# A two-layer attention trunk on one core: the first chunk's activations loaded already transposed, and the first loads reordered

## The chip, the cores and the metric

The kernel runs on one core of one Trainium2 chip. The metric is the device time of one execution in microseconds (us), less is better; the number to be predicted is the median of several runs.

## What is computed

The reference is a decoder trunk of two layers on 256 tokens of width 1024, in float32. Each layer does, in essence:

```
h = rms_norm(x, g_pre_mix[l])
parts = split(h @ w_in[l])                       # 2848 columns: q, k, v of two head groups, gates
o_nsa = nsa_mixer(...)                           # compressed, selected and window attention, gated
o_fox = fox_mixer(...)                           # attention with forgetting gates
x = x + rms_norm(concat(o_nsa, o_fox) @ w_out[l], g_post_mix[l])
h = rms_norm(x, g_pre_mlp[l])
x = x + rms_norm(square(relu(h @ w_up[l])) @ w_down[l], g_post_mlp[l])
```

For the products with `w_in` the kernel uses that the norm's factor is one number per token: it multiplies `(x * g) @ w_in`, and the factor is applied when a chunk's sums are read out of PSUM.

## The kernel before

**Tiling.** Tokens are two tiles t = 0, 1 of 128. The contraction dimension 1024 is eight slices k of 128. The columns of `w_in` are six chunks; the first that is worked on (chunk 0) has 512 columns, chunk 1 has 288, chunk 2 has 512, then three more. TensorE contracts over partitions, so the activations must stand with the contraction dimension on partitions: the tile pair `xT`, 128 x 8 x 256.

**Split precision.** Every operand is split into a part `hi` (float32r, made by ScalarE as a copy) and `lo` (VectorE, the value less `hi`). `mm3` (line 572) makes one product from three matmuls: hi·hi, hi·lo, lo·hi. Weights are split the same way in `Weights.get` (line 422): the load lands in `wraw`, ScalarE writes `whi`, VectorE writes `wlo`. There are RBUFS = 4 buffers for `wraw`, WBUFS = 7 each for `whi` and `wlo`, and 4 for the compression weights `w1`, which are used without a split.

**The start of layer 0.** Lines 515 to 534 issue the first loads, all on SyncE's queue (SP), in this order: the first half of token tile 0 of `x`; the identity (first 128 columns of `cst`); weight unit 0; `gcol`, the gain as eight columns; the second half of tile 0; units 1, 2, 3; the two halves of tile 1; units 4 to 7; the next columns of `cst`. A unit of chunk 0 is one k slice, 128 x 512 (`FIRSTS`, line 42). `first_xT(t)` (line 690) transposes tile t of `x` on TensorE, eight 128x128 transposes against the identity, four into each of two PSUM banks, multiplies by `gcol` into a tile `xg` (VectorE for t = 0, ScalarE for t = 1), and splits `xg` into `xT`. Some matmuls on a zeroed tile `warm` (line 537, WARM = 3, two instructions each) stand ahead of everything on TensorE.

Lines 1155 to 1161 run chunk 0 by token: all eight k of tile 0, then all eight of tile 1; `first_xT(1)` is recorded after the fourth product, the row factors `r_mix` after the eighth (`rstd_of_x`, line 601: ScalarE squares both halves of a tile of `x` with a sum, then a chain of small operations on VectorE and ScalarE gives one factor per token). `evac0` (line 736) reads chunk 0 out of PSUM with these factors into `kv_tok`, `kS` and `vS`. `row_scales` (line 1008) turns the factors into a row by four small matmuls. `gather_blocks` (line 805) transposes `kv_tok` and adds the position embedding on VectorE into `kstk` and `kstv`; `hidden_part` (line 822) multiplies these with `w1` in one stretch of 32 narrow matmuls, recorded behind the last quarter of chunk 2 (for k) and of chunk 3 (for v).

**Who sets the order.** The program is first recorded and then ordered by a planner, `Recorder.order` (line 241): for each engine it picks, at each point of its model's time, the ready operation with the smallest key (the place where it was recorded, or a key set by hand) for which buffers are free. A weight load has the key of the place 12 units earlier (`LOAD_LEAD`), a split that of one unit earlier. The order that comes out is fixed when the kernel is built, and each engine and SP's queue run it in order.

Of the kernel before, what the change touches and what calls it, by code (L numbers as in the profile page):

```python
# [18 lines left out]
F32 = mybir.dt.float32  # L19
F32R = mybir.dt.float32r  # L20
AF = mybir.ActivationFunctionType
OP = mybir.AluOpType
PSUM = bass.MemoryType.PSUM

P = 128
D = 1024
S = 256
NT = 2
# [5 lines left out]
LASTK = 4  # L34
LANE = 0.9
WAIT = 0.7
X1AT = 3
WARM = 3
RETILE = 145
SEQ = [(2, 0), (2, 1), (2, 2), (2, 3), (3, 0), (3, 1), (3, 2), (3, 3)]  # L40
EVKEY = 1
FIRSTS = [(i, i + 1) for i in range(8)]
UPK = 7
TOK, WBUFS, RBUFS = 6, 7, 4
LOAD_LEAD, SPLIT_LEAD = 12, 1
EPS = 1e-6
SEGS = ((0, 128, 0), (128, 384, 1))
GELU_C = 1.5957691216057308
# [1 line left out]
C_ID, C_ROPE, C_SID, C_TRI, C_MASK, C_CM, C_M01, C_ROW, C_SEL, C_END = np.cumsum(  # L50
    [0, 128, 64, 32, 256, 256, 32, 32, 8, 8]).tolist()
# [114 lines left out]
class Recorder:  # L166
    def __init__(self, nc, tc):
        self.nc, self.tc = nc, tc
        self.ops, self.fifo, self.key, self.hot, self.lane, self.group = [], {}, None, False, None, None
        for e in ("tensor", "vector", "scalar", "sync"):  # L170
            setattr(self, e, _Engine(self, e))

# [14 lines left out]
    def add(self, engine, name, args, kw):  # L187
        if self.group is not None:
            assert engine == "tensor"
            self.group.append((name, args, kw))  # L190
            return
        op = Op()
        op.engine, op.name, op.args, op.kw = engine, name, args, kw
        op.key = len(self.ops) if self.key is None else self.key
        if self.lane is not None and self.key is None:
            op.key = self.lane + LANE * (len(self.ops) - self.lane)
        op.urgent = self.hot
        views = []
        for _, a, k in args[2] if name == "stretch" else [(name, args, kw)]:
            views += [(i == 0, v) for i, v in enumerate(a) if isinstance(v, View)]  # L200
            views += [(i in ("out", "accum_out"), v) for i, v in k.items() if isinstance(v, View)]
        op.tile = _tile(op) if engine == "tensor" else None
        op.cost = _cost(op, views)
        deps = {}
        op.bufs = []
        for is_out, v in sorted(views, key=lambda x: x[0]):
            b, m = v.buf, v.mask()
            if b not in op.bufs:
                op.bufs.append(b)

            def against(entries):
                for o, p, q, bank in entries:
                    if o is not op and o not in deps and (
                            (bank and engine == "tensor") or
                            (p[0] < v.p[1] and v.p[0] < p[1] and (m & q).any())):
                        deps[o] = _latency(o, op)

            against(b.writes)
            entry = (op, v.p, m, is_out and b.psum and engine == "tensor")
            if is_out:  # L220
                against(b.reads)
                b.writes = [w for w in b.writes if not (
                    w[0] in deps and v.p[0] <= w[1][0] and w[1][1] <= v.p[1] and not (w[2] & ~m).any())]
                b.writes.append(entry)
            else:
                if b.psum:
                    for o, _, _, _ in b.reads:
                        if o.engine != engine and o is not op and o not in deps:
                            deps[o] = 130.0
                b.reads.append(entry)  # L230
        op.deps = deps
        for b in op.bufs:
            if not b.ops:
                self.fifo.setdefault(b.tag, []).append(b)
            b.ops += 1
        op.succs = []
        for d in deps:
            d.succs.append(op)
        self.ops.append(op)

    def order(self):
# [41 lines left out]
        while events:  # L283
# [5 lines left out]
            for e, ops in waiting.items():  # L289
                while busy[e] <= t:  # L290
# [35 lines left out]
                            count += 1  # L326
                            heapq.heappush(events, (best.end + (260 if b.psum else 150), count, b.tag))
                    for s in best.succs:
                        s.ready = max(s.ready, best.end + s.deps[best])
                        s.missing -= 1  # L330
                        if not s.missing:
                            waiting[s.engine].append(s)
                            count += 1
                            heapq.heappush(events, (s.ready, count, None))
# [74 lines left out]
class Weights:  # L409
# [12 lines left out]
    def get(self, i):  # L422
        nc, marks = self.nc, self.marks
        assert len(marks) == i
        marks.append(len(nc.ops))
        if i not in self.raw:
            nc.key = marks[max(i - LOAD_LEAD, 0)]
            self.load(i)
        kind, shape, src = self.units[i]
        raw = self.raw.pop(i)  # L430
        nc.key = None
        if kind == "raw":
            return raw
        nc.key = marks[max(i - SPLIT_LEAD, 0)]
        hi = self.tile([P] + shape, F32R, name="whi", tag="whi", bufs=WBUFS)
        lo = self.tile([P] + shape, F32R, name="wlo", tag="wlo", bufs=WBUFS)
        nc.scalar.activation(hi, raw, AF.Copy)
        nc.vector.tensor_sub(lo, raw, hi.bitcast(F32))
        nc.key = None
        return hi, lo  # L440

# [11 lines left out]
def trunk(nc, A, consts_in, out, sbp, pp):  # L453
    def tile(shape, dtype, name, tag=None, bufs=1):
        return nc.tile(sbp, shape, dtype, name, tag, bufs)

    def psum(tag):
        return nc.tile(pp, [P, 512], F32, tag, tag, {"acc": 2, "x": 2, "s": 3, "o": 1}[tag], psum=True)

    def small(shape, name, bufs=2):  # L460
        return tile(shape, F32, name=name, tag=name, bufs=bufs)
# [54 lines left out]
    cst = tile([P, C_END], F32, name="cst")  # L516
    ident = cst[:, C_ID:C_ID + P]
    xin = A["x"][0].rearrange("(t p) d -> t p d", p=P)
    gcol = tile([P, 8], F32, name="gcol")
    load_x = lambda t, n: nc.sync.dma_start(X[t][:, n * 512:n * 512 + 512], xin[t][:, n * 512:n * 512 + 512])  # L520
    load_x(0, 0)
    nc.sync.dma_start(cst[:, :P], consts_in[:, :P])
    W.load(0)
    nc.sync.dma_start(gcol, A["gcol"])
    load_x(0, 1)
    W.load(1)
    W.load(2)
    if len(FIRST) > 5:
        W.load(3)
    load_x(1, 0)  # L530
    load_x(1, 1)
    for i in range(3 + (len(FIRST) > 5), len(FIRST)):
        W.load(i)
    nc.sync.dma_start(cst[:, P:C_TRI], consts_in[:, P:C_TRI])


    warm = tokt("warm")
# [40 lines left out]
    def split(src, dst):  # L578
        nc.scalar.activation(dst[0], src, AF.Copy)
        nc.vector.tensor_sub(dst[1], src, dst[0].bitcast(F32))  # L580
# [106 lines left out]

    xT = new_xT()

    def first_xT(t):  # L690
        for n in range(2):
            ps = psum("s")
            for j in range(4):
                a = n * 512 + j * P
                nc.tensor.transpose(ps[:, j * P:j * P + P], X[t][:, a:a + P], ident)
            y = tokt("xg").rearrange("p (k n) -> p k n", k=4)
            for j in (0, 2):
                k = 4 * n + j
                if t:
                    for i in (j, j + 1):  # L700
                        nc.scalar.activation(y[:, i, :], ps[:, i * P:i * P + P], AF.Copy, scale=gcol[:, 4 * n + i:4 * n + i + 1])
                else:
                    nc.vector.tensor_mul(y[:, j:j + 2, :], ps[:, j * P:j * P + 2 * P].rearrange("p (k n) -> p k n", k=2),
                                         gcol[:, k:k + 2, None].to_broadcast([P, 2, P]))
                split(y[:, j:j + 2, :], [z[:, k:k + 2, t * P:t * P + P] for z in xT])

    first_xT(0)
    selr = tile([P, 8], F32R, name="selr")
    ident_r = tile([P, P], F32R, name="identr")
    r_mix = [None, None]  # L710
# [2 lines left out]
    for l in range(DEPTH):  # L713
        first = l == 0
        if first:
            params = load_params(0)
            nc.sync.dma_start(cst[:, C_TRI:], consts_in[:, C_TRI:])
        rows, bias, w2 = params
        smT = small([P, 37], "smT", 1)
        posT = {"k": smT[:, 0:16], "v": smT[:, 16:32]}  # L720
        b1T = smT[:, 32:36]
        b2k = smT[:, 36:37]
# [430 lines left out]


        if first:
            for n, _ in enumerate(in_chunk(0, evac0, by_token=True)):
                if n == X1AT:
                    first_xT(1)
                if n == 7:
                    for t in range(NT):  # L1160
                        r_mix[t] = rstd_of_x(t, "rm")
        else:

            for n, _ in enumerate(in_chunk(0, evac0, by_token=True)):
                if n == 6:
                    urgent(carry)
                    next(carry)
                    for t in range(NT):
                        r_mix[t] = rstd_of_x(t, "rm")
# [235 lines left out]
def layouts(a):  # L1405
# [7 lines left out]
    r["bias"] = np.concatenate([a["b_nsa_gate"], a["b_forget"], a["cmp_b2_v"]], axis=1)  # L1413
    w2 = [a[k].reshape(DEPTH, 2, P, 1, HD).transpose(0, 2, 1, 3, 4) for k in ("cmp_w2_k", "cmp_w2_v")]
    r["w2"] = np.stack([np.concatenate([x, x], axis=3) for x in w2], axis=2)
    r["gcol"] = a["g_pre_mix"][0].reshape(8, P).T
    r["consts"] = constants()
    return {k: np.ascontiguousarray(v) for k, v in r.items()}

# [15 lines left out]
```

## Time and profile before

| | |
|---|---|
| median of 3 runs | 648.28 us (647.78 to 648.38) |
| time of the profiled execution | 648.48 us |
| its span, first to last instruction | 646.7 us |
| TensorE busy | 634.1 us, 4032 matmuls |
| VectorE busy | 466.8 us |
| ScalarE busy | 358.7 us |
| read from HBM | 113.02 MB, 176 GB/s over the span |

The span lies inside the measured time; the rest (1.8 us) is around it. All times within the trace count from the start of the span. In its rows PE is TensorE's matmuls, PEld its weight loads, DVE is VectorE, ACT is ScalarE and SPq is SyncE's queue of DMA issues. An entry reads "out<-in", by the program's names of tiles; nearly every row bears the line of the planner's emitter, L348, so tiles tell the operations apart. Matmuls are pipelined: the duration of one is longer than the distance to the next, so the pace of TensorE is read from the starts.

### The profile page before, as it was taken

The numbers are of one execution on the slowest core, as the hardware profiler recorded it, in microseconds if no ns is written. First come the engines' busy times: TensorE is split into PE (matmuls) and PEld (weight loads), VectorE is DVE, ScalarE is ACT, GpSimd is POOL, SyncE is SP. The second block draws the span as 40 slices with busy tenths as digits, with TensorE's granted clock in tenths as the row PEclk, the third lists the DMA queues.
The fourth block names the chain that finished last, engine by engine and source line by source line (L and its number), as shares of the span: only waits on it lengthen the run. The fifth ranks groups of instructions, "written<-read, shape, count | busy, mean of one in ns | idle before, by whom it ended". The sixth has DMA issues, their size and how long they took to land.

```text
span 646.7 us, 10766 instructions
## 1 busy us (share of the span) xinstructions
PE 634.1 (98%) x4032; PEld 547.0 (85%) x4032; DVE 466.8 (72%) x1050; ACT 358.7 (55%) x681; POOL 0.2 (0%) x4
## 2 busy tenths in 40 slices
PE   8999999999999999999999999999999999999995
PEld 6788977778999899889888988777799899889984
DVE  5689999979965554555599799997987564555534
ACT  7557577654753553554366566764566543554332
POOL 0000000000000000000000000000000000000000
PEclk9999999999999999999999999999999999999999
DMA  8896915325775566655415973352277666555601
GB/s 260 272 325 211 326 50 178 116 66 192 236 256 193 176 186 196 188 181 186 121 51 159 329 223 104 115 170 76 74 240 245 193 193 189 181 185 195 189 7 65
DMA packets 53935, 114.75 MB, mean 177 GB/s; under 512 B 4274, under 2 KB 14716, under 8 KB 53884
## 3 DMA queue, kind: packets, MB, share of 16 engines
q1 hardware_dynamic: 53884, 114.08, 54.3%
q8 instruction: 31, 0.51, 0.3%
q14 instruction: 20, 0.16, 0.1%
HBM read 113.02 MB, written 1.05 MB: 176 GB/s over the span
## 4 chain that ended last, share of the span: by engine, by line
PE 93%; DMA 3%; DVE 2%; ACT 1%; issue 1%; SPq 0%; DVEq 0%
PE s L348 37%; PE acc L348 28%; PE x L348 24%; PE o L348 4%; DMA wraw<-in_w_in_dram 2%; DMA x<-in_x_dram 1%; DVE wlo L348 1%; ACT whi L348 0%; ACT xT L348 0%; DVE kstv L348 0%; SPq L348 0%; DVE kstk L348 0%; DVE xT L348 0%; ACT kS L348 0%; DVE m L348 0%
## 5 line engine op out<-in xcount | busy, mean ns | idle before, releaser
L348 DVE TENSOR_TENSOR wlo<-wraw,whi 128x1024 fp32r<-128x1024 f32 (+2 forms) x196 | 230.2, 1180 | 123.6 <-ACT whi L348 123.3
L348 ACT ACTIVATE whi<-wraw 128x1024 fp32r<-128x1024 f32 (+2 forms) x196 | 200.7, 1029 | 172.8 <-PE acc L348 74.1
L348 PE MATMUL s<-xT,whi 128*128 128x256 f32 x896 | 162.0, 283 | 0.0
L348 PEld LDWEIGHTS s<-xT,whi 128*128 128x128 f32 x896 | 139.9, 190 | 1.2
L348 PE MATMUL s<-xT,wlo 128*128 128x256 f32 x448 | 126.7, 283 | 0.0
L348 PE MATMUL acc<-whi,aT 128*128 128x512 f32 x256 | 89.3, 393 | 0.0
L348 PE MATMUL x<-whi,aT 128*128 128x512 f32 x256 | 88.9, 392 | 0.0
L348 PEld LDWEIGHTS s<-xT,wlo 128*128 128x128 f32 x448 | 85.3, 190 | 0.0
L348 PEld LDWEIGHTS acc<-whi,aT 128*128 128x128 f32 x256 | 48.1, 188 | 10.1
L348 PEld LDWEIGHTS x<-whi,aT 128*128 128x128 f32 x256 | 48.1, 188 | 9.8
L348 PE MATMUL acc<-wlo,aT 128*128 128x512 f32 x128 | 50.1, 391 | 0.0
L348 PE MATMUL x<-wlo,aT 128*128 128x512 f32 x128 | 50.0, 391 | 0.0
L348 ACT ACTIVATE pr<-pr,st 128x128 f32<-128x128 f32 (+1 forms) x96 | 42.7, 447 | 11.9 <-DVE st L348 11.8
L348 PE MATMUL acc<-xT,whi 128*128 128x256 f32 x256 | 49.2, 287 | 0.0
L348 PE MATMUL x<-whi,xT 128*128 128x512 f32 x128 | 42.7, 407 | 0.2 <-ACT xT L348 0.2
L348 PEld LDWEIGHTS acc<-xT,whi 128*128 128x128 f32 x256 | 40.6, 191 | 2.2 <-issue 1.2
L348 PE MATMUL acc<-whi,xT 128*128 128x512 f32 (+1 forms) x128 | 38.0, 364 | 0.0
L348 PE MATMUL acc<-xT,wlo 128*128 128x256 f32 x128 | 36.4, 285 | 0.0
L348 ACT ACTIVATE rl<-s 128x512 f32<-128x512 f32 x32 | 18.9, 590 | 22.3 <-PE s L348 22.3
L348 ACT ACTIVATE rl<-x 128x512 f32<-128x512 f32 x24 | 14.9, 620 | 27.1 <-PE x L348 18.1
L348 PEld LDWEIGHTS x<-whi,xT 128*128 128x128 f32 x128 | 24.7, 196 | 5.5 <-ACT xT L348 0.4
L348 PEld LDWEIGHTS acc<-wlo,aT 128*128 128x128 f32 x128 | 24.0, 188 | 5.5
(205 smaller groups left out, 926.9 us busy)
## 6 DMA issues: line engine op xcount, KB each, us to landing
wraw<-in_w_up_dram SPq DMA_DIRECT2D x64, 512.0 KB, 3.6
wraw<-in_w_down_dram SPq DMA_DIRECT2D x64, 512.0 KB, 3.8
wraw<-in_w_in_dram SPq DMA_DIRECT2D x36, 512.0 KB, 4.6
wraw<-in_w_out_dram SPq DMA_DIRECT2D x16, 512.0 KB, 4.5
w<-in_cmp_w_k_dram SPq DMA_DIRECT2D x8, 512.0 KB, 8.2
w<-in_cmp_w_v_dram SPq DMA_DIRECT2D x8, 512.0 KB, 8.6
wraw<-in_w_in_dram SPq DMA_DIRECT2D x8, 288.0 KB, 3.5
wraw<-in_w_in_dram SPq DMA_DIRECT2D x8, 256.0 KB, 4.8
```

The source lines that it names most:

```text
L348: getattr(getattr(self.nc, op.engine), name)(*[real(v) for v in args], **{k: real(v) for k, v in kw.items()})
```

## The change

Three things change together.

1. The host also gives `x` transposed: an input `xT` of 128 x (8 + 2048), the gain columns first, then the eight k slices of 256 tokens. `first_xT(k)` no longer uses TensorE or PSUM: ScalarE writes `hi` as the loaded slice times the gain, VectorE writes `lo` as the slice times the gain less `hi`. The plain `x` is still loaded, since the row factors and the residual use it.
2. The first loads go out as `xT` slice 0 (with the gain), unit 0, slices 1-2, unit 1, unit 2, slices 3-4, unit 3, slices 5-7, unit 4. `FIRSTS` makes units 2 to 4 of chunk 0 two k slices wide. The halves of `x` and the constants follow, and are not planned ahead of the last of these (`nc.after`). Parameters and the rest of `cst` are recorded after the twelfth product of chunk 0, and the loads of `w1` may not be planned earlier than six units ahead (`RIDE_LEAD`), in both layers.
3. Chunk 0 is no longer run by token: for each k, both tiles. The row factors are recorded after its twelfth product. The warm-up has four matmuls in place of three.

```diff
-X1AT = 3
-WARM = 3
+WARM = 4
-FIRSTS = [(i, i + 1) for i in range(8)]
+FIRSTS = [(0, 1), (1, 2), (2, 4), (4, 6), (6, 8)]
-LOAD_LEAD, SPLIT_LEAD = 12, 1
+LOAD_LEAD, SPLIT_LEAD, RIDE_LEAD = 12, 1, 6
...
-        deps = {}
+        deps = {} if self.after is None else {self.after: -1e9}
...
-                        s.ready = max(s.ready, best.end + s.deps[best])
+                        s.ready = max(s.ready, t, best.end + s.deps[best])
...
             nc.key = marks[max(i - LOAD_LEAD, 0)]
+            if self.units[i][0] == "raw":
+                nc.after = nc.ops[marks[max(i - RIDE_LEAD, 0)] - 1]
             self.load(i)
+            nc.after = None
...
-        nc.scalar.activation(hi, raw, AF.Copy)
-        nc.vector.tensor_sub(lo, raw, hi.bitcast(F32))
+        for j in range(shape[0]) if i < len(FIRSTS) else [slice(None)]:
+            nc.scalar.activation(hi[:, j], raw[:, j], AF.Copy)
+            nc.vector.tensor_sub(lo[:, j], raw[:, j], hi[:, j].bitcast(F32))
...
-    load_x(0, 0)
-    nc.sync.dma_start(cst[:, :P], consts_in[:, :P])
+    head = tile([P, 8 + S], F32, name="head", tag="tok", bufs=TOK)
+    gcol = head[:, 0:8]
+    xt = tile([P, 8, S], F32, name="xt", tag="gain")
+    xTk = [head[:, 8:]] + [xt[:, k, :] for k in range(1, 8)]
+    def load_xt(a, b):
+        nc.sync.dma_start(xt[:, a:b, :], A["xT"][:, 8 + a * S:8 + b * S].rearrange("p (k n) -> p k n", n=S))
+    nc.sync.dma_start(head, A["xT"][:, 0:8 + S])
     W.load(0)
-    nc.sync.dma_start(gcol, A["gcol"])
-    load_x(0, 1)
+    load_xt(1, 3)
     W.load(1)
     W.load(2)
...
+    load_xt(3, 5)
+    W.load(3)
+    load_xt(5, 8)
+    W.load(4)
+    nc.after = nc.ops[-1]
+    def load_rest():
+        for t in range(NT):
+            for n in range(2):
+                nc.sync.dma_start(X[t][:, n * 512:n * 512 + 512], xin[t][:, n * 512:n * 512 + 512])
+        nc.sync.dma_start(cst[:, :C_TRI], consts_in[:, :C_TRI])
+    load_rest()
+    nc.after = None
...
-    first_xT(0)
+    def first_xT(k):
+        hi, lo = (y[:, k, :] for y in xT)
+        nc.scalar.activation(hi, xTk[k], AF.Copy, scale=gcol[:, k:k + 1])
+        nc.vector.scalar_tensor_tensor(lo, xTk[k], gcol[:, k:k + 1], hi.bitcast(F32), op0=OP.mult, op1=OP.subtract)
...
-            params = load_params(0)
-            nc.sync.dma_start(cst[:, C_TRI:], consts_in[:, C_TRI:])
+            for k in range(8):
+                first_xT(k)
...
-            for n, _ in enumerate(in_chunk(0, evac0, by_token=True)):
-                if n == X1AT:
-                    first_xT(1)
-                if n == 7:
+            for n, _ in enumerate(in_chunk(0, evac0)):
+                if n == 11:
+                    nc.after = nc.ops[-1]
+                    rows, bias, w2 = load_params(0)
+                    nc.sync.dma_start(cst[:, C_TRI:], consts_in[:, C_TRI:])
+                    nc.after = None
                     for t in range(NT):
                         r_mix[t] = rstd_of_x(t, "rm")
```

The old `first_xT(t)` with its transposes is removed.

More of the change, by code (lines that the diff above doesn't have):

```diff
@@ L169, in __init__ @@
         self.ops, self.fifo, self.key, self.hot, self.lane, self.group = [], {}, None, False, None, None
+        self.after = None
         for e in ("tensor", "vector", "scalar", "sync"):
@@ L518, in trunk @@
     xin = A["x"][0].rearrange("(t p) d -> t p d", p=P)
-    gcol = tile([P, 8], F32, name="gcol")
-    load_x = lambda t, n: nc.sync.dma_start(X[t][:, n * 512:n * 512 + 512], xin[t][:, n * 512:n * 512 + 512])
-    load_x(0, 0)
-    nc.sync.dma_start(cst[:, :P], consts_in[:, :P])
+    head = tile([P, 8 + S], F32, name="head", tag="tok", bufs=TOK)
[5 more added lines that the diff above has]
+    nc.sync.dma_start(head, A["xT"][:, 0:8 + S])
     W.load(0)
-    nc.sync.dma_start(gcol, A["gcol"])
-    load_x(0, 1)
+    load_xt(1, 3)
     W.load(1)
     W.load(2)
[L528 to L534, printed above, removed]
+    load_xt(3, 5)
[10 more added lines that the diff above has]
+    nc.after = None
     warm = tokt("warm")
@@ L688, in trunk @@
     xT = new_xT()
[L690 to L705, printed above, removed]
-    first_xT(0)
+    def first_xT(k):
+        hi, lo = (y[:, k, :] for y in xT)
+        nc.scalar.activation(hi, xTk[k], AF.Copy, scale=gcol[:, k:k + 1])
+        nc.vector.scalar_tensor_tensor(lo, xTk[k], gcol[:, k:k + 1], hi.bitcast(F32), op0=OP.mult, op1=OP.subtract)
     selr = tile([P, 8], F32R, name="selr")
@@ L715, in trunk @@
         if first:
-            params = load_params(0)
-            nc.sync.dma_start(cst[:, C_TRI:], consts_in[:, C_TRI:])
-        rows, bias, w2 = params
+            for k in range(8):
+                first_xT(k)
+            params = None
         smT = small([P, 37], "smT", 1)
+        if not first:
+            rows, bias, w2 = params
         posT = {"k": smT[:, 0:16], "v": smT[:, 16:32]}
@@ L1415, in layouts @@
     r["w2"] = np.stack([np.concatenate([x, x], axis=3) for x in w2], axis=2)
-    r["gcol"] = a["g_pre_mix"][0].reshape(8, P).T
+    xt = a["x"][0].T.reshape(8, P, S).transpose(1, 0, 2).reshape(P, 8 * S)
+    r["xT"] = np.concatenate([a["g_pre_mix"][0].reshape(8, P).T, xt], axis=1)
     r["consts"] = constants()
```

## Prediction

> **What bounds the kernel now.** I read the page's totals first, then the chain of waits over the first 64 us, then the timeline of the start.
>
> ```profile
> span 646.7 us, 10766 instructions
> PE 634.1 (98%) x4032; PEld 547.0 (85%) x4032; DVE 466.8 (72%) x1050; ACT 358.7 (55%) x681; POOL 0.2 (0%) x4
> PE 93%; DMA 3%; DVE 2%; ACT 1%; issue 1%; SPq 0%; DVEq 0%
> ```
>
> TensorE is the bound: 93% of the chain is PE. A change to the start can save only what PE loses there. The timeline shows how much.
>
> ```profile
> 1.18 2.93 PE L348 MATMUL o<-warm 128*128 128x256 f32 x6 [1.18 <-DVE warm L348]
> 4.63 0.63 ACT L348 ACTIVATE whi<-wraw 128x512 fp32r<-128x512 f32 x1 [0.30 <-DMA wraw<-in_w_in_dram]
> 6.79 1.11 PE L348 MATMUL s<-cst,x 128*128 128x128 f32 x4 [1.83 <-DMA x<-in_x_dram]
> 7.56 0.78 PE L348 MATMUL x<-whi,xT 128*128 128x512 f32 x1
> 8.56 1.05 PE L348 MATMUL x<-whi,xT 128*128 128x512 f32 x2
> 9.41 0.73 PE L348 MATMUL x<-wlo,xT 128*128 128x512 f32 x1
> 12.51 0.75 PE L348 MATMUL x<-whi,xT 128*128 128x512 f32 x2
> 18.96 0.62 PE L348 MATMUL x<-whi,xT 128*128 128x512 f32 x2
> 19.41 0.39 PE L348 MATMUL x<-wlo,xT 128*128 128x512 f32 x1
> 23.23 0.39 PE L348 MATMUL x<-whi,xT 128*128 128x512 f32 x1
> 24.43 0.88 PE L348 MATMUL s<-cst,kv_tok 128*128 128x128 f32 x6 [0.51 <-ACT kv_tok L348]
> 26.18 0.40 PE L348 MATMUL acc<-wlo,xT 128*128 128x288 f32 x1 [0.29 <-DVE wlo L348]
> ```
>
> The first product of chunk 0 starts at 7.56, the last ends at 23.62 (23.23 + 0.39): 16.06 us for 48 products of 512 columns. At 19 us two of them take 0.45 (18.96 to 19.41), 0.226 each, so 48 would take 10.85. The rest is transposes, waits and a slow clock: at 8.56 two take 0.85 (to 9.41), 0.427 each. The pair at 12.51 spans 0.75 where that at 8.56 spans 1.05: the clock rises there, some 11 us after the first warm-up.
>
> The bytes come next; columns are the busy times, PEclk, DMA share and GB/s.
>
> ```profile
> 2.00:4.00 2.00, 2.00 (x6) 1.40 (x6) 0.00 (x0) 0.59 (x3) 0.00 (x0) 1.00 0.91 271
> 4.00:6.00 2.00, 0.96 (x5) 0.56 (x3) 1.16 (x4) 1.51 (x6) 0.00 (x0) 1.00 0.83 222
> 6.00:8.00 2.00, 1.21 (x5) 1.21 (x6) 1.08 (x4) 1.28 (x4) 0.00 (x0) 1.00 0.83 287
> 8.00:12.00 4.00, 4.00 (x14) 2.91 (x13) 3.91 (x13) 3.15 (x10) 0.00 (x0) 1.00 1.00 347
> 25.00:28.00 3.00, 2.71 (x19) 2.29 (x18) 2.97 (x12) 2.03 (x4) 0.00 (x0) 1.00 0.32 63
> 28.00:34.00 6.00, 6.00 (x63) 4.65 (x61) 5.85 (x16) 2.87 (x4) 0.00 (x0) 1.00 0.74 243
> 40.00:50.00 10.00, 10.00 (x59) 8.85 (x58) 6.21 (x14) 4.75 (x8) 0.00 (x0) 1.00 1.06 374
> ```
>
> DMA is near full from 2 us on, at only 222 to 287 GB/s until 8 us and near 350 after. What matters is the order of the bytes: at 11.13 two transfers of w1 go out, not needed before 32 us, and chunk 0's seventh weight unit then keeps ACT waiting until 19.13.
>
> ```profile
> 11.13 0.93 SPq L348 DMA_DIRECT2D w<-in_cmp_w_k_dram  x2
> 19.13 0.63 ACT L348 ACTIVATE whi<-wraw 128x512 fp32r<-128x512 f32 x1 [1.40 <-DMA wraw<-in_w_in_dram]
> 32.04 1.93 PE L348 MATMUL o<-w,kstk 128*32 128x256 f32 x32
> 34.57 1.01 SPq L348 DMA_DIRECT2D w<-in_cmp_w_v_dram  x2
> ```
>
> **The change part by part.** Durations that I need:
>
> ```profile
> L348 DVE TENSOR_TENSOR wlo<-wraw,whi 128x512 fp32r<-128x512 f32 x8 | 5.4, 689 | 4.1 <-ACT whi L348 4.1
> L348 ACT ACTIVATE whi<-wraw 128x512 fp32r<-128x512 f32 x8 | 5.1, 632 | 1.9 <-DMA wraw<-in_w_in_dram 1.7
> L348 ACT ACTIVATE xT<-xg 128x256 fp32r<-128x256 f32 x8 | 3.2, 417 | 0.2 <-DVE xg L348 0.2
> L348 ACT ACTIVATE kS<-x,rsqrt 128x256 f32<-128x256 f32 x1 | 0.5, 467 | 0.0
> L348 DVE SCALAR_TENSOR_TENSOR mg<-mg,rsqrt,xo 128x256 f32<-128x256 f32 x24 | 10.0, 480 | 0.2
> ```
>
> The new `hi` of a slice is the 417 ns copy with a scale per partition; the nearest row with such a scale took 467. Bounds 0.42 and 0.47, I take 0.47. The new `lo` is of the 480 ns kind. So a k slice costs ACT 0.63 + 0.47 = 1.10 us, DVE 0.69 + 0.48 = 1.17, DMA 0.39 MB (0.26 of weights, 0.13 of xT), 1.1 us at 350 GB/s, and PE 6 x 0.226 = 1.36. Once the clock is up, PE is the slowest of the four, by little.
>
> *First product (-3.0).* Now two transfers of 0.40 MB together stand ahead of it. In before, unit 0 was complete after 0.59 MB; the DMA rows give 0.54 MB from 2.0 to 4.0 us (2 x 271; I take 0.04 for the time before), and ACT was released at 4.63, so 0.6 later. With the same rates 0.40 MB are in at 3.3, released at 3.9; `whi` ends at 4.55. The xT slice lands earlier and is split in that time. PE starts at 4.55 in place of 7.56.
>
> *First to last product (-3.4).* Same rates, 0.6 added: unit 1 (0.92 MB) at 6.1, unit 2 (1.45) at 8.0, unit 3 (2.23) at 10.4, unit 4 (3.15) at 13.0. After a landing, `wlo` of the first slice is ready 1.3 us later and that of the second 0.7 after it. PE then ends slice k=1 at 8.7 at latest if the clock is up by 8, k=2 at 10.4 (waiting for `wlo` at 9.45), k=3 at 11.8, k=4 at 13.2, and k=7 at 17.2: 12.65 us in place of 16.06. The slow clock costs nothing up to 8 us, since bytes hold PE then. The clock: in before PE was idle for 1.83 us up to 6.79 and then slow until 12.5; now warm-ups (eight of 0.427 from 1.18 to 4.6) join the products without such a hole.
>
> [...]
>
> *The 16 transposes* (eight of them between the first and last product) and the `xg` steps are inside these two terms. SP's nine issues, 0.46 each by the row at 11.13, take it to about 5 us; the bytes are slower, so they cost nothing.
>
> *Row factors, moved out of the stretch (+0.6).* Two pairs of small matmuls and the transpose of `rows` ran between products of chunk 0; now they come behind.
>
> ```profile
> 14.87 0.18 PE s L348
> 20.03 0.22 PE s L348 x2
> 24.77 0.08 DVE vS L348
> 34.15 5.25 DMA wraw<-in_w_in_dram
> 40.93 8.95 DMA wraw<-in_w_in_dram
> 62.79 1.21 PE o L348 x19
> ```
>
> 2 x 0.22 + 0.18 = 0.62.
>
> *Behind chunk 0 (+0.8).* In before, PE lost about 1.3 of the 2.56 us from 23.62 to 26.18 (nine transposes of 0.11, half the pair at 20.03, and two products of 0.226 x 288/512 = 0.13 are work). Now `x` (1.05 MB) and constants (0.11 MB) come between unit 4 and chunk 1: its first unit (0.30 MB) is complete at 4.61 MB, 16.6 us, released 17.2, `whi` at about 18.0: a wait of 0.8.
>
> ```profile
> 16.44 0.64 ACT L348 ACTIVATE rl<-x 128x512 f32<-128x512 f32 x1
> 16.96 0.20 ACT L348 ACTIVATION_READ_ACCUMULATOR rl<-x 128x1 f32 x1
> 17.76 0.41 DVE L348 SCALAR_TENSOR_TENSOR rsqrt<-rsqrt 128x1 f32<-128x1 f32 x2 [0.32 <-ACT rsqrt L348]
> ```
>
> In before the factor of tile 1 was there at 18.17, 1.0 after its last square, and chunk 0 ended 5 us later. Now tile 1 of `x` lands at about 16.0; two squares with their reads (2 x 0.84) and that 1.0 put it at 18.7, behind the end of chunk 0. Queued behind it are `evac0` on ACT, then gather transposes on PE and `kstk` on DVE; chunk 1 (16 x 3 x 0.13 = 6.4 us) can cover them if the planner puts it first. I take 1.3 again: 2.1 in place of 1.3. Bounds: 1.0 (no new wait) and 4 (the factors hold PE from 17.2 to evac0 of both tiles, at 21).
>
> *Later.* The row of before from 24.77 to 34.15 in the chain is DVE work (rope, `wlo`, `kst`) of 9.4 us. It begins when tile 0 is evacuated, then about 20, so it moves 4.8 us: like PE. w1 no longer goes ahead of chunk weights, so less stands in front of chunk 3; but the 32-matmul stretch on w1 that filled PE at 32.04 is not at hand that early: up to 1.9 us given away, or nothing if chunk 2 is there. I take nothing, and keep 1.9 for the range. That the planner orders all else anew I price at plus or minus 0.8, the two waits in the rows at 24.43 and 26.18 together.
>
> Sum: -3.0 - 3.4 + 0.6 + 0.8 = -5.0 us. Against the profiled execution's 648.48 that is 643.5; the median of the runs is 0.2 lower: **643.3**.
>
> **The rivals.**
>
> *The clock stays slow until 12.5 as before.* For: it is the one release the trace shows. Against: the hole before 6.79 is gone. Then the slices take 2.56 each, k=2 ends at 12.3, chunk 0 at 19.2, 2.0 later; the 0.8 of waiting for chunk 1 goes. Time 644.5.
>
> *The late row factors hold the next stage.* ACT has the four squares, both evacuations and chunk 1's splits between 14 and 22; if squares go first, `whi` is late, and the DVE chain of 9.4 us starts nearer 22.5. For: DVE is busy 5.85 of 6 us from 28 to 34. The gain at the end is about 2.3 and not 5: 646.0, up to 648 with the 1.9 of the missing filler.
>
> *DMA takes the place of PE: slower.* Between 34.15 and 49.88 the chain runs through two stretches of DMA, at 374 GB/s in the last ten. The change adds 1.05 MB. If the queue stays as full as now and its idle time is not used, whatever waits at 49.88 comes 1.05 MB / 374 GB/s = 2.8 us later and the head start is lost: 651.1. It is decided by the idle DMA from 25 to 34: 3 x (374 - 63) + 6 x (374 - 243) = 1.7 MB unused. If over 1.05 MB of that is used, it doesn't bind. For use: part of it is due to buffers that DVE frees, and DVE starts earlier. Also, w1 for v, 2.1 MB at 34 to 39 and used at 62.8, need not come before chunk 3.
>
> [...]
>
> *The change doesn't do what it says:* unit 4 needs the buffer of unit 0, and all of `x` stands behind it on SP. That buffer is free at 5.2, about when SP gets there; worth 0.5 at most, inside the range.
>
> **How the numbers follow.** Forecast 62%: 643.3, own range 641 to 645. Slow clock 12%. Late factors 16%, of which 5 end within 0.2%. DMA bound 10%, of which 2 within. 0.2% is 1.3 us, about what a measurement can tell from no change (the runs spread over 0.6). So faster 85, same 7, slower 8. The range, 8 in 10: low end 640.9, the forecast with no new wait behind chunk 0 (-1.1), the planner in its favour (-0.8) and 0.5 for earlier bytes; the high end 646.9 takes in the slow clock and most of the late factors and leaves out DMA.
>
> **What would show it.** First product near 4.5; 0.226 spacing from 8 us or earlier; last product of chunk 0 near 17; first chunk-1 product near 18; a PE wait of under 2.5 us in all between 17 and 27; no DMA in the chain after 34, and the MLP stages unchanged in length. Wrong would be: PE idle behind `kv_tok` or `rsqrt` for over 3 us, or `whi` waiting for DMA past 45.

## The result, and the profile after

| | |
|---|---|
| median after | 649.38 us (13 runs, 647.83 to 650.48) |
| median before, in the same comparison | 647.78 us (13 runs, 647.46 to 649.14) |
| ratio, 95% interval | 1.0021 [1.0012, 1.003] |
| profiled execution after (its span) | 648.69 us (646.9) |
| predicted | 643.3 us, 640.9 to 646.9 |

The forecast was 5 us faster. It came out 0.2% slower, outside the range, and the interval leaves out 1. Every ratio below is against the kernel before on the same chip.

The totals on the page of after hardly differ from those of before: less work on PE, but a smaller share of PE in the chain.

```profile
span 646.9 us, 10723 instructions
PE 633.5 (98%) x4018; PEld 545.0 (84%) x4018; DVE 466.0 (72%) x1046; ACT 354.6 (55%) x673; POOL 0.2 (0%) x4
PE 91%; DVE 4%; DMA 2%; ACT 1%; issue 1%; SPq 0%; DVEq 0%; ACTq 0%
```

The timeline of PE in after, at the start:

```profile
1.21 3.78 PE L348 MATMUL o<-warm 128*128 128x256 f32 x8 [1.21 <-DVE warm L348]
4.60 1.25 PE L348 MATMUL x<-whi,xT 128*128 128x512 f32 x2
6.50 0.63 PE L348 MATMUL x<-wlo,xT 128*128 128x512 f32 x1
6.92 0.60 PE L348 MATMUL x<-whi,xT 128*128 128x512 f32 x1
7.93 0.73 PE L348 MATMUL x<-whi,xT 128*128 128x512 f32 x2 [0.40 <-ACT whi L348]
8.65 0.50 PE L348 MATMUL x<-wlo,xT 128*128 128x512 f32 x1
8.99 0.39 PE L348 MATMUL x<-whi,xT 128*128 128x512 f32 x1
9.22 0.39 PE L348 MATMUL x<-wlo,xT 128*128 128x512 f32 x1
...
17.64 0.39 PE L348 MATMUL x<-whi,xT 128*128 128x512 f32 x1
18.01 0.51 PE L348 MATMUL acc<-whi,xT 128*128 128x288 f32 x2
...
25.06 0.62 PE L348 MATMUL x<-whi,xT 128*128 128x512 f32 x2
27.25 0.40 PE L348 MATMUL acc<-wlo,xT 128*128 128x288 f32 x1 [1.57 <-DVE wlo L348]
```

The start did what it was meant to do. The first product begins at 4.60 (7.56 in before), the last one of chunk 0 at 17.64 (23.23), and chunk 1 follows at 18.01. So the gain is made and must be lost later. To find where, take the start of the same operation in both traces at four places: the first product of layer 0's MLP, of layer 1's chunk 0, of layer 1's MLP, and the last product of all. Timeline of PE, before:

```profile
143.50 0.39 PE L348 MATMUL s<-whi,xT 128*128 128x512 f32 x1
...
326.63 0.39 PE L348 MATMUL x<-whi,xT 128*128 128x512 f32 x1
...
457.59 0.39 PE L348 MATMUL s<-whi,xT 128*128 128x512 f32 x1
...
639.58 0.40 PE L348 MATMUL acc<-whi,aT 128*128 128x512 f32 x1
```

and after:

```profile
138.60 0.40 PE L348 MATMUL s<-whi,xT 128*128 128x512 f32 x1
...
322.95 0.39 PE L348 MATMUL x<-whi,xT 128*128 128x512 f32 x1
...
456.39 0.40 PE L348 MATMUL s<-whi,xT 128*128 128x512 f32 x1
...
639.65 0.39 PE L348 MATMUL acc<-whi,aT 128*128 128x512 f32 x1
```

The differences are -4.90, -3.68, -1.20 and +0.07; their size, where they are negative, is called the lead below. At the end of layer 0's attention the forecast of -5.0 stands. One trace is good to about 0.6 us here: the eight traces of this document with after's layer 0 reach its MLP between 138.30 and 139.47, the five with before's between 143.00 and 144.10. Then the MLP of layer 0 gives back 1.22 us, the attention of layer 1 gives back 2.48, and the MLP of layer 1 gives back 1.27.

**The MLP stages** have one PE wait each. From 138 to 324 us the waits of PE (engine and tile, what was waited for, us in all, times, longest) are this row in after, and the same row in before:

```profile
PE s L348 <- DVE xT L348: 0.7, 1, 0.7
```

So the loss is no wait: it is pace. The first and the last of the 48 products of one down block (layer 1), before and then after:

```profile
550.33 0.40 PE L348 MATMUL x<-whi,aT 128*128 128x512 f32 x1
...
561.10 0.40 PE L348 MATMUL acc<-whi,aT 128*128 128x512 f32 x1
```

```profile
549.61 0.39 PE L348 MATMUL x<-whi,aT 128*128 128x512 f32 x1
...
560.52 0.40 PE L348 MATMUL acc<-whi,aT 128*128 128x512 f32 x1
```

47 distances in 10.77 us are 229.1 ns each; in 10.91 us, 232.1. The durations in the rows (0.39, 0.40) hide this, since products overlap; only the starts tell. There are 768 such products (moving `whi` or `wlo`, stationary `aT`) in the two layers: 768 x 3.0 ns = 2.3 us, nearly all of the 1.22 + 1.27.

**Layer 1's attention** has new waits. Timeline rows of before (SP's queue, DVE, PE):

```profile
64.08 1.81 SPq L348 DMA_DIRECT2D w<-in_cmp_w_k_dram  x3
344.04 1.77 DVE L348 TENSOR_TENSOR kstk<-s,smT 64x120 f32<-64x120 f32 x7
351.10 1.93 PE L348 MATMUL o<-w,kstk 128*32 128x256 f32 x32
```

and of after (SP's queue, DVE, PE):

```profile
313.90 0.46 SPq L348 DMA_DIRECT2D w<-in_cmp_w_k_dram  x1
337.03 0.47 SPq L348 DMA_DIRECT2D w<-in_cmp_w_k_dram  x1
339.76 1.10 SPq L348 DMA_DIRECT2D w<-in_cmp_w_k_dram  x2
340.35 1.77 DVE L348 TENSOR_TENSOR kstk<-s,smT 64x120 f32<-64x120 f32 x7
348.87 0.50 PE L348 MATMUL x<-wlo,xT 128*128 128x512 f32 x1 [0.70 <-DVE wlo L348]
356.81 1.93 PE L348 MATMUL o<-w,kstk 128*32 128x256 f32 x32
417.43 1.23 DVE L348 TENSOR_TENSOR xo<-x,gains 128x1024 f32<-128x1024 f32 x1 [1.61 <-DMA gains<-in_g_pre_mlp_dram]
420.00 0.52 PE L348 MATMUL s<-cst,pr 128*128 128x128 f32 x3 [0.94 <-DVE st L348]
```

In before, layer 1's four loads of `w1` for k go out from 64.08 on (the fourth at 66.50), during layer 0's attention. In after three of the four go out at 337 to 340, among the loads of layer 1's own chunks. In before the stretch of 32 products on `w1` starts 5.3 us after `kstk` is complete (345.81). In after `kstk` is complete 3.7 earlier (342.12), and the stretch comes 14.7 behind it. PE meanwhile waits 0.70 for `wlo`. Later VectorE stands 1.61 us in front of `xo`, waiting for a load of gains, with the softmax's `st` queued behind it, and PE loses 0.94 more.

### The profile page after: what moved, and what is told of

It is laid out like the page before. It is cut to its first block, busy times and chain, and to the rows that moved or that the text cites. A ratio compares the mean times of both kernels' runs of the same rounds, so it can differ in the third digit from the quotient of the medians.

```text
span 646.9 us, 10723 instructions
## 1 busy us (share of the span) xinstructions
PE 633.5 (98%) x4018; PEld 545.0 (84%) x4018; DVE 466.0 (72%) x1046; ACT 354.6 (55%) x673; POOL 0.2 (0%) x4
## 4 chain that ended last, share of the span: by engine, by line
PE 91%; DVE 4%; DMA 2%; ACT 1%; issue 1%; SPq 0%; DVEq 0%; ACTq 0%
PE s L348 36%; PE acc L348 28%; PE x L348 23%; PE o L348 4%; DMA gains<-in_g_pre_mlp_dram 1%; DMA wraw<-in_w_in_dram 1%; DVE kstv L348 1%; DVE kstk L348 1%; ACT xT L348 0%; SPq L348 0%; DVE wlo L348 0%; ACT whi L348 0%; ACT rl L348 0%; DVE xT L348 0%; DVE kx L348 0%
## 5 line engine op out<-in xcount | busy, mean ns | idle before, releaser
L348 ACT ACTIVATE pr<-pr,st 128x128 f32<-128x128 f32 (+1 forms) x96 | 42.7, 445 | 17.4 <-DVE st L348 17.2
```

The source lines that it names most:

```text
L348: getattr(getattr(self.nc, op.engine), name)(*[real(v) for v in args], **{k: real(v) for k, v in kw.items()})
```

## The experiments

Two losses, two questions: why do 512-column products start later after one another, and is holding `w1` back the reason for layer 1's order?

**Alignment of tiles (theory A) and the hold (theory C).** The change moved most tiles in SBUF; in after many start at 32 modulo 64 bytes. (Addresses are those of the compiled programs, in bytes within a partition.) The pace is that of the block of 48 products shown above, which stands in every trace. The first kernel puts after's tiles at multiples of 64:

```diff
-    one_t = small([P, 1], "one", 1)
+    one_t = small([P, 16], "one", 1)[:, 0:1]
```

> The changed kernel with one small constant tile widened from 4 to 64 bytes per partition; the instructions and their order on every engine are the same, but nearly all tiles behind it stand 32 bytes higher, so that the split weights start at multiples of 64 bytes as in the kernel before (in the changed kernel they start at 32 above one). Theory A (the addresses cost what the MLP stages gave back): the mean distance of the 512-column matmuls in the down products goes from 232 back to 229 ns, each MLP block is 1.2 us shorter, the attention and output products about 0.6 in all, and the time is 2.5 to 3.5 us under the changed kernel's: 646.0 to 646.9, ratio to before 0.997 to 0.9985. Rival B (other traffic or the clock slowed these matmuls): same pace as in the changed kernel, ratio 1.001 to 1.003.

Measured: 648.99 us, 1.0014 [1.0, 1.0028]; the block takes 10.91 us, 232.1 ns, as in after.

The second moves before's `whi`, `wlo`, `xT` and `aT` to 32 modulo 64:

```diff
-    gcol = tile([P, 8], F32, name="gcol")
+    gcol = tile([P, 16], F32, name="gcol")[:, 0:8]
```

> The kernel before with the gain columns' tile widened from 32 to 64 bytes per partition: same instructions and order, but the split weights, xT, aT and oT start 32 bytes above a multiple of 64 bytes. Theory A: the down products' 512-column matmuls go from 229 to 232 ns, and the time rises by 2.5 to 3.5 us, ratio 1.004 to 1.0055. Rival B: no change, ratio 0.9985 to 1.0015.

Measured: 648.55 us, 1.0004 [0.9992, 1.0016]; 10.77 us, 229.1 ns, as in before. Theory A falls on both sides.

The third is after with `w1` held back in layer 0 only:

```diff
-            if self.units[i][0] == "raw":
+            if self.units[i][0] == "raw" and i < len(self.units) // DEPTH:
                 nc.after = nc.ops[marks[max(i - RIDE_LEAD, 0)] - 1]
```

> The changed kernel, but loads of the compression weights are held back to six units ahead in layer 0 alone; in layer 1 they may go as early as before. Theory C (in layer 1 the held-back loads take the narrow stretch away that filled TensorE while the low parts of chunk 2 were being made, and shift the gains' load into a wait): the wait of 0.9 us near 348 us goes, the wait of 1.1 us near 419 us probably too, and the time is 1.0 to 2.5 us under the changed kernel's, ratio 0.998 to 1.0005. Rival D (the order that the planner finds in layer 1 is luck, not this rule): ratio 1.001 to 1.004, with waits of the same sum elsewhere.

Measured: 646.34 us, 0.9972 [0.9959, 0.9985]. That is 0.0049 or 3.2 us under after, more than the 2.5 at most expected. The loss in layer 1's attention is gone: the lead is 3.42 us at its start and 3.49 at its end, and PE has no wait in it. The pace is still that of after (10.92 us for the block). Both edits together:

> The changed kernel with both: the constant tile widened to 64 bytes and the loads held back in layer 0 alone. Theories A and C together: the 4.9 us that the changed kernel is ahead at the start of the first MLP stay to the end, less 0 to 1; time 643.0 to 644.5, ratio 0.9925 to 0.995. If only A holds: 646 (0.998). If only C: 647 to 648 (0.999 to 1.0005). If neither: 1.002.

Measured: 646.23 us, 0.997 [0.996, 0.9981], like the third. So the hold in layer 1 is one cause, and the pace is left as another. The traces of all runs agree on the first: layer 1's attention takes 132.9 to 134.1 us in the three kernels that hold `w1` back there, and 130.8 to 130.9 in the six changed kernels that do not (before: 130.96).

**PSUM banks (theory E).** In before the tiles `s` are allocated ahead of `x` and have banks 1 to 3, `x` has 4 and 5; in after `x` has 1 and 2. One warm-up product, written to another tag, exchanges this (after with the hold in layer 0, tag `s`; before, tag `x`):

```diff
     for i in range(WARM):
+        if i == WARM - 1:
+            ps = psum("s")
         nc.tensor.matmul(ps[:, :S], warm[:, :P], warm[:, :S], start=True, stop=True)
```

> The kernel after with w1 held back in layer 0 only (646.34 us, ratio 0.9972 when it ran), and with one thing more: the last of the four warm-up products writes a PSUM tile of tag s instead of o. Every engine's instructions and their order stay as they are; what changes is that the three s tiles get PSUM banks 1 to 3 and the two x tiles banks 4 and 5, as in the kernel before (without it x has 1 and 2, s has 3 to 5). Theory E (the slower 512-column products of the down stages, 232.5 ns a start against 229, come from which PSUM banks x and acc lie in): the down products go back to 228 to 230 ns, the lead over the kernel before stays at -4.5 to -5.0 us through the MLP of layer 0 and is -4 to -5 us at the end, 643.3 to 644.0 us, ratio 0.9930 to 0.9945. Rival F (the pace hangs on something else that the change moved: where the weights lie against each other in SBUF, or when the loads and the splits run): 232 to 233 ns as before, lead -2.3 us at the end, 646 to 646.6 us, ratio 0.9965 to 0.998.

> The kernel before with one edit: the last of its three warm-up products writes a PSUM tile of tag x instead of o. Instructions and their order stay; x gets banks 1 and 2 and s gets 3 to 5, as in the kernel after. Theory E: its down products start 232 to 233 ns apart instead of 229, the two MLP stages are 1.1 to 1.3 us longer each, and 0.4 to 0.6 us more goes in the other stages: 650.2 to 651.0 us, ratio 1.0035 to 1.005. Rival F: 229 ns, within 0.1 % of the kernel before.

Measured: 646.1 us, 0.9966 [0.9952, 0.9981], 232.1 ns; and 648.41 us, 1.0 [0.999, 1.0009], 229.1 ns. Theory E falls too.

**The distance from `aT` to the weights (theory G).** The kernels whose pace had stayed had one thing in common: each kept its parent's distance from `whi` to `aT`. (`wlo` lies at the same place as `whi` modulo 4096, and all buffers of a tag are 4096 apart.) Before has 448 bytes modulo 4096, after 384. The small tile `csm` lies between; padding it moves `aT` alone among the tiles that the down products read:

```diff
-            sm = small([P, NT, 8], "csm", 1)
+            sm = small([P, NT + 2, 8], "csm", 1)[:, :NT]
```

> The kernel after with w1 held back in layer 0 only, and the small tile csm padded by 64 bytes; the tiles behind it, aT among them, then lie 64 bytes further on, and whi, wlo and xT where they were. From whi to aT it is then 448 bytes modulo 4096, as in the kernel before, and not 384 as in the kernel after (the realigned and the shifted kernel had kept the distance of their own parent). Instructions and orders are unchanged. Theory G (the down products are slower because aT, from which their weights are loaded, and whi and wlo, which stream past, lie at another distance in SBUF): 229 ns instead of 232.5 ns, the lead is kept through both MLP stages, 643.3 to 644.0 us, ratio 0.9930 to 0.9945. Rival H (it is the 22 instructions that PE has fewer ahead of them, or the time at which loads and splits run, and no place of a tile): 232.5 ns, 646 to 646.6 us, ratio 0.9965 to 0.998.

And the other way round, in before, `csm` allocated first, so that `whi` comes 64 bytes nearer to `aT`:

```diff
-            for op in self.order():
+            order = self.order()
+            for b in [b for op in order for b in op.bufs if b.label == "csm"][:1]:
+                b.real = b.pool.tile(b.shape, b.dtype, name=b.name, tag=b.label, bufs=b.bufs)
+            for op in order:
```

> The kernel before with csm allocated first, so that whi, wlo and xT lie 64 bytes further on and aT stays: 384 bytes modulo 4096 from whi to aT, as in the kernel after. Instructions and orders are unchanged. Theory G: down products 232.5 ns apart instead of 229, 2.2 to 3 us more in all, 650.2 to 651.2 us, ratio 1.0033 to 1.005. Rival H: 229 ns, within 0.1 %.

Measured: 643.81 us, 0.9934 [0.9919, 0.9949], and 650.8 us, 1.0036 [1.0022, 1.0049]. The same block of 48 products, timeline of PE, first in after with the hold in layer 0 and `aT` 64 bytes further:

```profile
545.80 0.40 PE L348 MATMUL x<-whi,aT 128*128 128x512 f32 x1
...
556.57 0.40 PE L348 MATMUL acc<-whi,aT 128*128 128x512 f32 x1
```

then in before with `aT` 64 bytes nearer:

```profile
552.20 0.39 PE L351 MATMUL x<-whi,aT 128*128 128x512 f32 x1
...
563.11 0.40 PE L351 MATMUL acc<-whi,aT 128*128 128x512 f32 x1
```

10.77 and 10.91 us: the two paces have changed places, 229.1 and 232.1 ns. The program is the same instruction for instruction; only addresses differ. Theory G holds. The first of the two, at the four places of above and at the stretch on `w1`:

```profile
139.07 0.40 PE L348 MATMUL s<-whi,xT 128*128 128x512 f32 x1
...
322.23 0.40 PE L348 MATMUL x<-whi,xT 128*128 128x512 f32 x1
...
346.66 1.93 PE L348 MATMUL o<-w,kstk 128*32 128x256 f32 x32
...
453.07 0.39 PE L348 MATMUL s<-whi,xT 128*128 128x512 f32 x1
...
635.05 0.40 PE L348 MATMUL acc<-whi,aT 128*128 128x512 f32 x1
```

Its lead over before is 4.43, 4.40, 4.52 and 4.53 us: what the start gains is kept to the end, and the stretch on `w1` is back at 346.66.

**Is each loss there alone, and what does the hold do in layer 0?** Three kernels follow: after with `csm` padded and nothing else; the version of 643.81 us with 128 bytes in place of 64; and that version without any hold (`RIDE_LEAD = 99`):

> The kernel after as it is (w1 held back in both layers), with csm padded by 64 bytes and nothing else. If the two losses are separate and add up: the 2.4 us of the slower down products go (and some tenths in the layers' other 512-column products), the 2.5 us of layer 1's attention stage stay. 646.5 to 647.2 us, ratio 0.9970 to 0.9985, lead -4.4 to -4.9 us at the start of layer 1 and -1.8 to -2.2 us at the end. If the pad also repairs layer 1's order, 643.5 to 644.5 us.

> As the version of 643.81 us (w1 held back in layer 0 only, aT 64 bytes further), with aT 128 bytes further instead: 512 bytes modulo 4096 from whi to aT. It asks by which distance the pace goes. Theory G1 (a distance that is a multiple of 128 bytes costs, as 384 did): 232 to 233 ns, 646 to 646.6 us, ratio 0.9965 to 0.998. Theory G2 (by the distance modulo 512 or more; the products x<-whi,xT, whose distance is 0 modulo 4096, start 227 ns apart in both kernels): 226 to 229 ns, 642.3 to 644 us, ratio 0.991 to 0.9945.

> The version of 643.81 us with w1 held back in neither layer, so that layer 0's w1 loads are no longer tied to the products six units before them. Theory: holding them back in layer 0 does little, since the wait of 1.74 us at 25.3 us is for wlo and the DVE work ahead of it; within 0.15 % of 643.8 us, ratio 0.992 to 0.995. Rival: the eight w1 loads of 0.5 MB go ahead of the second chunk's weights on the queue and push its products back by 2 to 6 us: 646 to 650 us, ratio 0.996 to 1.002, with PE waits for weights between 18 and 40 us.

Measured: 646.61 us, 0.998 [0.9969, 0.9991]; 642.1 us, 0.991 [0.9894, 0.9926]; 645.18 us, 0.9962 [0.9947, 0.9977].

The losses add up, to within the intervals: from after's 1.0021 the hold undone in layer 1 takes 0.0049, the pad 0.0041, both together 0.0087 (5.6 us). The hold in layer 0 is useful, against my theory: without it the version is 0.0028 (1.8 us) slower, and its trace has the loss before the MLP of layer 0, which begins 1.69 us later than the 139.07 above:

```profile
140.76 0.40 PE L348 MATMUL s<-whi,xT 128*128 128x512 f32 x1
```

With 128 bytes (512 modulo 4096) the same block is faster than either kernel had it, in 10.68 us or 227.2 ns:

```profile
544.28 0.40 PE L348 MATMUL x<-whi,aT 128*128 128x512 f32 x1
...
554.96 0.39 PE L348 MATMUL acc<-whi,aT 128*128 128x512 f32 x1
```

So a distance that is a multiple of 128 bytes isn't bad in itself (G1 falls): 384 gives 232.1, 448 gives 229.1, 512 gives 227.2. All fourteen traces have one of these distances, and their pace goes by it: six with 384, six with 448, two with 512, in kernels of both families and with either alignment to 64 bytes. Other distances were not tried. This version, 642.1 us, beats both kernels. The last run gives before the 512 bytes, by the `csm` pad of 64:

> The kernel before with csm padded by 64 bytes: 512 bytes modulo 4096 from whi to aT instead of 448, instructions and orders unchanged. It prices the distance without the change. If the pace goes by the distance alone: down products 226 to 228 ns apart instead of 229, 1.8 to 2.2 us less in all, 645.7 to 646.5 us, ratio 0.9965 to 0.9975, and the change itself (with w1 held back in layer 0 only) is then worth 4 to 4.5 us at equal distance. If the 512 bytes do it only with the places that tiles have in the kernel after: 229 ns, within 0.1 % of the kernel before.

Measured: 646.98 us, 0.9977 [0.9966, 0.9989], a little less gain than expected, with 227.2 ns in the next block (10.68 us from 572.57). By the pace alone, 768 x 1.9 ns = 1.5 us; I had expected other products to gain as well, but those on `oT`, which has the place of `aT`, went only from 230.0 to 229.7 ns. At equal distance the change, with the hold in layer 0 only, is worth 0.9977 - 0.991 = 0.0067, or 4.3 us.

## Why the prediction was wrong

- *First product (-3.0)*: 7.56 to 4.60, -2.96. Right.
- *First to last product (-3.4)*: the last one starts 5.59 earlier, so this term was -2.63. Chunk 0 ended at 18.03 (17.64 + 0.39) and not at 17.2. The sum counts on the clock being up by 8; no run shows that time. What the trace shows in its place is a pace: products start 0.42 apart up to 6.92 (from 6.50) and 0.23 apart from 8.99 (to 9.22). That the slow pace is a slow clock is my reading, as the profile's clock column is at 1.00 in both stretches; what ends it is not shown. From 8.99 to 17.64 the 38 distances are 0.228 each, so all of the 0.8 was lost before 8.99. About 0.4 of it lies in the three distances from 7.93 to 8.99, 0.35 each in place of 0.226; the rest in the late start of slice k=1 at 7.93, with a wait of 0.40 for `whi` ahead of it. Why those three stand at 0.35 is not shown. The rival of a slow clock until 12.5 is ruled out by these rows.
- *Row factors (+0.6)* and *Behind chunk 0 (+0.8)*: together the lead shrank from 5.59 to 4.90 up to the MLP, 0.7 in place of 1.4. The wait is there (1.57 at 27.25, under the 2.5 allowed), but its place is `wlo`, which VectorE reaches only behind `kstv` and `kx`. The factor of tile 1 was complete at 19.77, where 18.7 was estimated, but PE has no other wait between 18.01 and 27.25. Timeline of VectorE in after:

```profile
24.32 1.48 DVE L348 TENSOR_TENSOR kstv<-s,smT 64x128 f32<-64x128 f32 x6
25.84 0.69 DVE L348 TENSOR_TENSOR kx<-s,kx 128x512 fp32r<-128x512 f32 x1
26.45 1.88 DVE L348 TENSOR_TENSOR wlo<-wraw,whi 128x576 fp32r<-128x576 f32 x2
```

- These errors cancel: -4.90 measured, -5.0 predicted. That the sum is so close is luck: two terms were off by 0.7 to 0.8, in opposite directions.
- *Later ("I take nothing", the planner at ±0.8)*: **the first step that failed.** It looked for the missing `w1` stretch in layer 0 alone. The diff holds `w1` back in both layers, and layer 1 has nothing to gain from that, as its start was not touched. There it cost 2.48 us in the trace (3.2 in the medians), shown by undoing it in layer 1 alone. In before these loads had gone out 250 to 270 us earlier, and without the hold they do so again (from 63.00). The two waits (0.70 and 0.94) are seen; the remaining 0.8 is spread over the stage and not told apart.
- *"The MLP stages unchanged in length"*: **the second.** Nothing in them was edited, yet they lost 2.5 us, as new tiles moved the distance between `aT` and the weights. That this is the cause is shown in both directions. What in the chip makes it so is not: no run separates the two operands that PE reads from what other engines read and write meanwhile.
- *DMA takes the place of PE*: did not come; after's chain has no load of weights behind 34. The `gains` load in the chain at 410 belongs to the planner's order of layer 1: with the hold in layer 0 only, `xo` doesn't wait, and the lead stays.

Without the two losses the result is near the forecast: 643.81 against 643.3, with a lead of 4.53 us at the end where 5.0 was predicted.

## What to carry to other kernels

Check for each rule of a diff which parts of the program it reaches, and price it where it has no purpose; a hold that helps one layer (1.8 us here) cost 2.5 to 3.2 in the next. When a change adds or reorders tiles, compare the start-to-start distance of the main products in untouched stages, not their durations: 3 ns on 768 products undid half of a gain. An address can be tried alone by padding a small tile, and here it was worth 1.5 us even in the kernel before, which is bound by TensorE (93% of its chain).

## What the runs showed of the hardware

The pace of back-to-back 128x512 products, each with its own weight load, depended on where the stationary operand's tile lies against the streaming one's, with the same instructions: 232.1, 229.1 and 227.2 ns at 384, 448 and 512 bytes modulo 4096. The operands' alignment to 64 bytes and the PSUM banks made no difference (232.1 and 229.1 ns with either changed, as without; changed in the kernel before, they left its time at 1.0004 and 1.0). Among the tiles that the products read, moving the one from which the weights are loaded, and nothing else, changed the pace from 232.1 to 229.1 and 227.2 ns; what in the chip does this is not shown. Three distances are no rule: whether the pace repeats with some power of two of bytes is not shown.
